# Two engines that read one PSUM buffer: both of ScalarE's copies ahead of VectorE's, small transfers spread over tiles, a mean computed later

## The chip, the cores and the metric

The kernel runs on one core of a Trainium2 chip. The metric is the device time of one execution, in microseconds (us). A core has the engines TensorE (PE, with PEld for its weight loads), VectorE (DVE), ScalarE (ACT), GpSimd (POOL) and SyncE (SP), which issues transfers. They run side by side, each in its own order, and wait for one another by semaphores.

## The reference

One layer of an encoder, on two sequences of 2048 tokens with 1024 features, with shared weights:

```
h = rms_norm(x, norm_w);  proj = h @ w_in
q_a, k_a, v_a, g_a, q_b, k_b, v_b, g_b = split(proj)     # 512 128 128 512 | 512 512 512 512
q_a, k_a = partial_rope(rms_norm(q_a)), partial_rope(rms_norm(k_a))
o_a = windowed_gqa_sink(q_a, k_a, v_a, sink_a) * silu(g_a)   # 8 q heads, 2 kv heads, +-128 tokens
q_b, k_b = rms_norm(q_b), rms_norm(k_b)
o_b = neighbourhood_attn(q_b, k_b, v_b, rpb_b) * silu(g_b)   # 8 heads, 64-wide grid, 8 x 16 window
x = x + concat(o_a, o_b) @ w_out
y = x + (p @ w_ple) * sigmoid(x @ w_ple_gate)
```

All of it is in fp32.

## The kernel before

Matmul operands are kept as two rounded parts: ScalarE writes the high part ("hi") of a value, VectorE the rest ("lo" = value − hi), and a product is three matmuls, hi·hi, hi·lo and lo·hi. So most results in PSUM are read by both engines: ScalarE copies or scales them into a high part, VectorE subtracts that high part from the same PSUM buffer.

The span has three stages. Stage A (0 to some 790 us) takes 32 tiles of 128 tokens, 16 of each sequence; `f` numbers them. For each tile `proj_a(f)` projects k and v (PSUM `pk`), q (`pq`) and the gate (`pg`), and two calls of `unit_a` (one for each kv head) do the windowed attention: scores `sc`, softmax (`mx`, `nm` and the exponentials L219 into `s`), transposes `pt` into PSUM and from there into `pr`, products `po`, and `fin`, which transposes the gate into `pgt`, adds the two halves of `po` into `ot` (L537 and L538) and multiplies (L539). Stage B (790 to some 1860 us) takes 64 tiles, `f` from 32 to 95: two halves of the heads, two sequences, 16 tiles each. `proj_b(f)` projects q and k together (`pqk`) and v and the gate together (`pvg`), `keys_b` transposes the keys into PSUM `pktb` and writes four blocks of `ks_b` from it, `prep_b` and `split_q` make `q1b` and `q`, and `unit_b` does the attention: `scb`, exponentials, `ptb` into `p_t`, products `pob`, and `fin` with `pgtb` and `o_tb` (added up on POOL at L694, multiplied on DVE at L697). Its products come in four blocks, `x` = 0 to 3. Behind stage B come the output projection and, in stage C, the gate's products, which the change does not touch.

TensorE's order is set by hand: `pinned` links every matmul and transpose to the one before, and `PLAN_A` and `PLAN_B` say at which share of the projection's work a step of the attention is put in. The order on the other engines is made by the scheduler from the program and its dependencies; SP's transfers and a few operations are kept in program order. Each engine then runs its list strictly in order, and an instruction that waits holds those behind it.

PSUM buffers come from pools by tag: three for the projections, three shared by `sc`, `scb`, `pt`, `ptb`, `pgt` and `pgtb`, and two shared by `pkt`, `pqt`, `po` and their counterparts of stage B. A new tile of a tag waits until the one that held its buffer has been read: the third `ptb` of a tile takes the buffer of `pgtb`, so it waits for `o_tb` L697.

`square(f, i)` squares one half of x for the row means: the load `stn<-x_n`, ScalarE's square in place (L292) and, behind the second half, VectorE's two small operations `ms` (L300) and `ee` (L302). `split(f, i)` makes the two parts of x itself (`xr` on ScalarE L278, then POOL L279). Both are called while TensorE is in an earlier tile's projection. `regroup(s)` runs after the last tile of a sequence in stage A: it writes the 2048 means to DRAM (L471) and reads them back in the order of stage B's tiles in 16 small transfers (L474); `stats_b(s)` turns them into scales. `raw` (L461) is a step of `combine`, which prepares sums of weights for stage C on POOL, one operation in some of stage B's tiles.

Of the kernel before, what the change touches and what calls it, by code (L numbers as in the profile page):

```python
# [11 lines left out]
F32 = mybir.dt.float32  # L12
# [7 lines left out]
DM = 1024  # L20
# [64 lines left out]
def emit(ctx, tc, io):  # L85
# [108 lines left out]
    def project(ps, xr, w, cost):  # L194

        for k in range(KT):
            for i, (a, b) in enumerate(((0, 0), (0, 1), (1, 0))):
                mm(ps, xr[:, a, k, :], w(k, b), k == 0 and i == 0, k == KT - 1 and i == 2)
                yield cost, k == KT - 1 and i == 2
# [32 lines left out]

    def split_q(pqt, q1, q2):

        for e in range(2):
            a, z = 64 * e, 64 - 64 * e
            nc.scalar.copy(q1[e][a:a + 64], pqt[a:a + 64])
            nc.vector.tensor_tensor(out=q2[e][a:a + 64], in0=pqt[a:a + 64], in1=q1[e][a:a + 64].bitcast(F32),
                                    op=ALU.subtract)
            nc.gpsimd.tensor_copy(q1[e][z:z + 64], q1[e][a:a + 64])  # L240
        return q1, q2


# [39 lines left out]
    def square(f, i):  # L283

        if f >= 2 * NT:
            return
        if i == 0:
            stats[f] = (ap.tile([128, 12], F32, tag="ssq", name="ssq", bufs=3),
                        ap.tile([128, 1], F32, tag="ee", name="ee", bufs=3))
        ssq, ee = stats[f]  # L290
        xn = staged.pop(("n", f, i))
        nc.scalar.activation(xn, xn, AF.Square, accum_out=ssq[:, 10 + i:11 + i])  # L292
        if f > 1:
            load_next()
        if i == 1:
            for dst, src in copies[:CP] if f >= 2 else ():
                tc.keep_in_program_order(nc.sync.dma_start(dst, src))
                copies.pop(0)
            ms = ms_a[:, f:f + 1]
            nc.vector.tensor_scalar(out=ms, in0=ssq[:, 10:11], scalar1=ssq[:, 11:12], scalar2=1.0 / DM,  # L300
                                    op0=ALU.add, op1=ALU.mult)
            nc.vector.tensor_scalar(out=ee, in0=ms, scalar1=EPS, scalar2=EPS * EPS, op0=ALU.mult, op1=ALU.add)  # L302

    def big(shape, dt, name):
        return ap.tile(shape, dt, tag="big", name=name, bufs=3)
# [60 lines left out]
    def keys_a(kt, t):  # L366
        pkt = ptile([128, 128], "ms", "pkt")
        tr(pkt, kt[:, 0:2, :].rearrange("p h d -> p (h d)"))
        c = slice(128 * t, 128 * t + 128)
        for e in range(2):  # L370
            a, z = 64 * e, 64 - 64 * e
            nc.scalar.activation(ks_a[a:a + 64, e, c], pkt[a:a + 64], AF.Copy, scale=wk[a:a + 64, 0:1])
            nc.vector.scalar_tensor_tensor(out=ks_a[z:z + 64, e, c], in0=pkt[a:a + 64], scalar=wk[a:a + 64, 0:1],
                                           in1=ks_a[a:a + 64, e, c].bitcast(F32), op0=ALU.mult, op1=ALU.subtract)

    def proj_a(f):
# [2 lines left out]
        ka = 22 if f in last else KA  # L379
        pk = ptile([128, 256], "pj", "pk")  # L380
        yield from project(pk, xr, lambda k, b: wx[:, k, b, :], 112)
        sq2 = ap.tile([128, 512], F32, tag="sq", name="sq2", bufs=2)
        nc.scalar.activation(sq2[:, :128], pk[:, 0:128], AF.Square)
        nc.vector.tensor_reduce(out=ssq[:, 8:10], in_=sq2[:, :128].rearrange("p (h d) -> p h d", d=HD),
# [56 lines left out]
        held[f] = q, gs, y  # L441
        if t == NT - 1:
            regroup(s)
        if f == NT + 4:
            stats_b(0)
        yield 0, False

# [21 lines left out]
    def regroup(s):  # L469
        c = slice(NT * s, NT * s + NT)  # L470
        nc.sync.dma_start(ms_d[s * SEQ:(s + 1) * SEQ].rearrange("(t p) -> p t", p=128), ms_a[:, c])  # L471
        rows = ms_d.rearrange("(r k c) -> r k c", k=4, c=16)
        for i in range(NT * s, NT * s + NT):
            nc.sync.dma_start(ms_b[:, i:i + 1], rows[8 * (i // 4):8 * (i // 4) + 8, i % 4, :].rearrange("r c -> c r"))  # L474

    def stats_b(s):
        c = slice(NT * s, NT * s + NT)
# [14 lines left out]
    def unit_a(f, kv):  # L492
        s, t = divmod(f, NT)
        _, gs, y = held[f]
        k0, k1 = max(0, t - 1), min(NT, t + 2)
        n = 128 * (k1 - k0)
        m0 = 128 * (k0 - t + 1)
        sm, prs, got = sm_tiles(), [], {}

        def sc(i):  # L500
            ps = ptile([128, 512], "sc", "sc")
            for j, q in enumerate(qs[f]):
                mm(ps[:, :n], q[kv][:, 128 * i:128 * i + 128], ks_a[:, kv, 128 * k0:128 * k1], j == 0, j == 1)
            softmax(i, ps, n, mask[:, m0:m0 + n], sm)
            if i == 3:
                got["g2"] = exps(sm, n, y[:, 11:12], gs[:, 256 * kv:256 * kv + 256],
                                 (snk[:, 0, 4 * kv:4 * kv + 4], snk[:, 1, 4 * kv:4 * kv + 4]))

        def pt(j):
            if j >= k1 - k0:  # L510
                return
            pt = ptile([128, 4, 128], "pt", "pt")
            for i in range(4):
                tr(pt[:, i, :], sm["s"][i][:, 128 * j:128 * j + 128])
            pr = main.tile([128, 2, 512], F32R, tag="p_t", name="pr", bufs=3)
            pf = pt.rearrange("p h q -> p (h q)")
            nc.scalar.copy(pr[:, 0], pf)
            nc.vector.tensor_tensor(out=pr[:, 1], in0=pf, in1=pr[:, 0].bitcast(F32), op=ALU.subtract)  # L518
            prs.append(pr)

        def po(j):
            if j == 0:
                got["po"] = ptile([128, 512], "ms", "po")
            if j < k1 - k0:
                v = vv[:, k0 + j, kv].rearrange("p a d -> p (a d)")
                for i in range(2):
                    mm(got["po"], v, prs[j][:, i], j == 0 and i == 0, k0 + j == k1 - 1 and i == 1)

        def fin(_):
            pgt = ptile([128, 2, 128], "sc", "pgt")  # L530
            for i in range(2):
                tr(pgt[:, i, :], got["g2"][:, 128 * i:128 * i + 128])
            ot = ap.tile([128, 2, 128], F32, tag="ot", name="ot", bufs=2)
            ph2 = got["po"].rearrange("p (i e q) -> p e i q", e=2, q=128)
            for e in range(2):
                a, z = 64 * e, 64 - 64 * e
                nc.scalar.copy(ot[a:a + 64], ph2[z:z + 64, e])  # L537
                nc.vector.tensor_tensor(out=ot[a:a + 64], in0=ph2[a:a + 64, e], in1=ot[a:a + 64], op=ALU.add)  # L538
            nc.vector.tensor_tensor(out=ot, in0=pgt, in1=ot, op=ALU.mult)  # L539
            nc.sync.dma_start(oa_d[s].rearrange("(i p) q -> p i q", p=128)[:, 2 * kv:2 * kv + 2, 128 * t:128 * t + 128],  # L540
                              ot)
        return {"sc": sc, "pt": pt, "po": po, "fin": fin, "prep": lambda _: nxt(f) if kv else None}
# [3 lines left out]
    def keys_b(kt, b, cb):  # L546
        pkt = ptile([128, 2, 16, 8], "ms", "pktb")
        for i in range(2):
            tr(pkt[:, i].rearrange("p c r -> p (c r)"), kt[:, 2 * i:2 * i + 2, :].rearrange("p h d -> p (h d)"))
        for i in range(2):  # L550
            for e in range(2):
                a, z = 64 * e, 64 - 64 * e
                hi, lo = (ks_b[i][p:p + 64, 8 * b:8 * b + 8, e, 16 * cb:16 * cb + 16].rearrange("p r c -> p c r")
                          for p in (a, z))
                nc.scalar.activation(hi, pkt[a:a + 64, i], AF.Copy, scale=wk[a:a + 64, 1:2])  # L555
                nc.vector.scalar_tensor_tensor(out=lo, in0=pkt[a:a + 64, i], scalar=wk[a:a + 64, 1:2],  # L556
                                               in1=hi.bitcast(F32), op0=ALU.mult, op1=ALU.subtract)

    def proj_b(f):
        half, st = divmod(f - 2 * NT, 2 * NT)  # L560
        s, j = divmod(st, NT)
        b, cb = divmod(j, 4)
        if f == 2 * NT + 4:
            stats_b(1)
        if not ks_b:
            ks_b.extend(big([128, 32, 2, 64], F32R, f"ks_b{i}") for i in range(2))
# [26 lines left out]
        for i, c in enumerate(project(pv, xr, lambda k, b: w_vg[k][:, b, :], 215)):  # L593
# [3 lines left out]
            if i == (KB if f not in last else 10):  # L597
                if f < 2 * NT + 2:
                    pending.append((kt, b, cb))
                else:  # L600
                    keys_b(kt, b, cb)
        v = ap.tile([128, 4, 2, HD], F32R, tag="sq", name="vb", bufs=2)
        vp = pv[:, 0:256].rearrange("p (h d) -> p h d", d=HD)
        nc.scalar.activation(v[:, :, 0, :], vp, AF.Copy, scale=rs_b[:, st:st + 1])
        nc.vector.scalar_tensor_tensor(out=v[:, :, 1, :], in0=vp, scalar=rs_b[:, st:st + 1],
                                       in1=v[:, :, 0, :].bitcast(F32), op0=ALU.mult, op1=ALU.subtract)
        for w, (c0, ncol) in COL_WIN.items():
            lo, hi = max(c0, 16 * cb), min(c0 + ncol, 16 * cb + 16)
            if lo < hi:
                nc.sync.dma_start(v_d[half, s, w][8 * b:8 * b + 8, lo - c0:hi - c0].rearrange("r c h a d -> c r (h a d)"),  # L610
                                  v[8 * (lo - 16 * cb):8 * (hi - 16 * cb)].bitcast(F32).rearrange("p h a d -> p (h a d)"))
        gs = qg[:, 1].rearrange("p h d -> p (h d)")
        nc.scalar.activation(gs, pv[:, 256:512], AF.Tanh, scale=hr_b[:, st:st + 1])
        nc.vector.scalar_tensor_tensor(out=gs, in0=gs, scalar=1.0, in1=pv[:, 256:512], op0=ALU.add, op1=ALU.mult)
        held[f] = qg[:, 0], gs
        next(combining, None)
# [526 lines left out]
```

## Time and profile before

| | |
|---|---|
| median of three runs | 2642.3 us (2638.67, 2642.3, 2643.25) |
| profiled execution | 2645.63 us |
| its span | 2643.9 us |
| granted clock of TensorE in it | 0.988 of full speed |

The span is what the profiler saw from the first to the last instruction; the profiled execution's own time is 1.7 us above it. "Busy" is the time in which an engine executes; waits are put down to what released them. A row of the timeline has the start in us from the beginning of the span, the duration, the engine, the line, the operation, output and inputs, and in brackets the idle time ahead of it. The lines are quoted in the prediction.

### The profile page before, as it was taken

The numbers are of one execution on the slowest core, as the hardware profiler recorded it, in microseconds if no ns is written. First come the engines' busy times: TensorE is split into PE (matmuls) and PEld (weight loads), VectorE is DVE, ScalarE is ACT, GpSimd is POOL, SyncE is SP. The second block draws the span as 40 slices with busy tenths as digits, with TensorE's granted clock in tenths as the row PEclk, the third lists the DMA queues.
The fourth block names the chain that finished last, engine by engine and source line by source line (L and its number), as shares of the span: only waits on it lengthen the run. The fifth ranks groups of instructions, "written<-read, shape, count | busy, mean of one in ns | idle before, by whom it ended". The sixth has DMA issues, their size and how long they took to land.

```text
span 2643.9 us, 46984 instructions
## 1 busy us (share of the span) xinstructions
PE 2559.5 (97%) x16080; PEld 2274.8 (86%) x16080; DVE 1927.4 (73%) x5702; ACT 1419.9 (54%) x3327; POOL 794.5 (30%) x996
## 2 busy tenths in 40 slices
PE   7999989999999999999899999999979998999999
PEld 5888878888877888888788888888979998999999
DVE  5887778878797788888888888888675548555554
ACT  5666656666665566666666666666431124222322
POOL 3332323333232333333333332221132323223321
PEclk9999999999999999999999999999989999999999
DMA  6323322111133455555755554457575455233221
GB/s 203 106 94 108 106 75 77 61 59 49 53 101 117 157 174 170 180 177 158 235 164 168 188 175 145 152 156 220 172 244 176 151 172 179 76 104 101 81 78 48
DMA packets 230974, 357.50 MB, mean 135 GB/s; under 512 B 38320, under 2 KB 115760, under 8 KB 225584
## 3 DMA queue, kind: packets, MB, share of 16 engines
q1 hardware_dynamic: 230736, 354.51, 42.7%
q8 instruction: 128, 2.10, 0.3%
q14 instruction: 110, 0.90, 0.1%
HBM read 266.33 MB, written 105.92 MB: 141 GB/s over the span
## 4 chain that ended last, share of the span: by engine, by line
PE 67%; DVE 13%; ACT 9%; DMA 5%; issue 3%; POOL 2%; SPq 1%; DVEq 0%; POOLq 0%; ACTq 0%
PE pqk L189 12%; PE pvg L189 12%; PE acca L973 11%; PE accc L973 8%; ACT s L219 4%; PE pob L189 4%; PE pple L189 3%; PE scb L189 3%; PE ptb L192 3%; DMA stn<-x_n 3%; PE pout L189 3%; DVE s L204 2%; DVE pr L518 2%; PE pq L189 2%; PE pg L189 1%
## 5 line engine op out<-in xcount | busy, mean ns | idle before, releaser
L189 PE MATMUL pvg<-wb,xr 128*128 128x512 f32 x1536 | 457.8, 405 | 0.0
L189 PE MATMUL pqk<-wa,xr 128*128 128x512 f32 x1536 | 436.8, 407 | 0.0
L219 ACT ACTIVATE s<-s,nm 128x384 f32<-128x384 f32 (+4 forms) x512 | 306.3, 600 | 242.0 <-DVE nm L215 183.1
L189 PEld LDWEIGHTS pqk<-wa,xr 128*128 128x128 f32 x1536 | 266.8, 189 | 37.2
L189 PEld LDWEIGHTS pvg<-wb,xr 128*128 128x128 f32 x1536 | 269.1, 190 | 31.6
L279 POOL TENSOR_TENSOR xr<-stx,xr 128x512 fp32r<-128x512 f32 x192 | 248.1, 1300 | 143.1 <-ACT xr L278 125.5
L189 PE MATMUL pg<-wb,xr 128*128 128x512 f32 x768 | 232.4, 409 | 1.5 <-ACT wb L142 0.9
L189 PE MATMUL pq<-wa,xr 128*128 128x512 f32 x768 | 224.3, 406 | 5.4 <-DVE wa L143 2.8
L229 POOL TENSOR_TENSOR g<-qg,rd 128x256 f32<-128x256 f32 x64 | 39.2, 613 | 492.8 <-DVE rd L227 478.9
L973 PE MATMUL acca<-opd,s 128*128 128x256 f32 x1344 | 171.1, 290 | 16.6 <-DVE r L992 13.1
L973 PEld LDWEIGHTS acca<-opd,s 128*128 128x128 f32 x1344 | 169.2, 199 | 17.1 <-DVE r L992 10.1
L189 PEld LDWEIGHTS pq<-wa,xr 128*128 128x128 f32 x768 | 142.1, 192 | 30.3 <-DVE wa L143 3.8
L204 DVE CUSTOM_DVE_ANT_0 s<-scb,bias 128x288 f32<-128x288 f32 (+3 forms) x256 | 141.9, 555 | 30.0 <-PE scb L189 25.2
L667 ACT CAST p_t<-ptb 96x384 fp32r<-96x384 f32 (+3 forms) x256 | 129.8, 508 | 51.4 <-PE ptb L192 49.7
L189 PEld LDWEIGHTS pg<-wb,xr 128*128 128x128 f32 x768 | 137.1, 189 | 23.0 <-DVE wb L143 1.8
L668 DVE TENSOR_TENSOR p_t<-ptb,p_t 96x384 fp32r<-96x384 f32 (+3 forms) x256 | 149.0, 584 | 9.1 <-ACT p_t L667 6.2
L555 ACT ACTIVATE ks_b<-pktb,wk 64x128 fp32r<-64x128 f32 x256 | 124.9, 489 | 47.9 <-DVE ks_b L556 41.6
L189 PEld LDWEIGHTS pob<-p_t,vw 128*128 128x128 f32 (+2 forms) x832 | 132.8, 189 | 18.9 <-ACT wa L142 0.5
L556 DVE SCALAR_TENSOR_TENSOR ks_b<-pktb,wk,ks_b 64x128 fp32r<-64x128 f32 x256 | 115.0, 449 | 39.7 <-ACT ks_b L555 33.1
L939 POOL TENSOR_TENSOR opd<-sum,opd 128x1024 fp32r<-128x1024 f32 x28 | 70.2, 2508 | 235.9 <-ACT opd L925 235.9
L189 PE MATMUL pob<-p_t,vw 128*128 128x256 f32 (+2 forms) x832 | 140.4, 282 | 0.1
L204 DVE CUSTOM_DVE_ANT_0 s<-sc,mask 128x384 f32<-128x384 f32 (+1 forms) x256 | 136.2, 534 | 0.2
(197 smaller groups left out, 5878.6 us busy)
## 6 DMA issues: line engine op xcount, KB each, us to landing
stx<-x_b SPq DMA_DIRECT2D x128, 256.0 KB
vw<-v_d SPq DMA_DIRECT2D x112, 256.0 KB
stx<-x_a SPq DMA_DIRECT2D x64, 256.0 KB
stn<-x_n SPq DMA_DIRECT2D x64, 256.0 KB
v_d<-vb SPq DMA_DIRECT2D x64, 256.0 KB
x1r<-x_d SPq DMA_DIRECT2D x16, 1024.0 KB
y_t<-r SPq DMA_DIRECT2D x64, 256.0 KB
v_d<-vb SPq DMA_DIRECT2D x96, 128.0 KB
```

Source lines behind the costliest of these rows:

```text
L189: pinned(nc.tensor.matmul(out, lhsT, rhs, start=start, stop=stop))
L192: pinned(nc.tensor.transpose(out, in_, ident))
L204: nc.vector.tensor_tensor_reduce(out=s[:, :n], in0=ps[:, :n], in1=bias, scale=1.0, scalar=-3.0e38, op0=ALU.add, op1=ALU.max, accum_out=sm[ ...
L219: nc.scalar.activation(ss[i][:, :n], ss[i][:, :n], AF.Exp, bias=nm[:, i:i + 1], accum_out=den[:, i:i + 1])
L279: nc.gpsimd.tensor_tensor(out=lo, in0=raw, in1=hi.bitcast(F32), op=ALU.subtract)
L518: nc.vector.tensor_tensor(out=pr[:, 1], in0=pf, in1=pr[:, 0].bitcast(F32), op=ALU.subtract)
L555: nc.scalar.activation(hi, pkt[a:a + 64, i], AF.Copy, scale=wk[a:a + 64, 1:2])
L556: nc.vector.scalar_tensor_tensor(out=lo, in0=pkt[a:a + 64, i], scalar=wk[a:a + 64, 1:2], in1=hi.bitcast(F32), op0=ALU.mult, op1=ALU.subtract)
L667: nc.scalar.copy(p_t[:kc, :nch, 0], pf)
L668: nc.vector.tensor_tensor(out=p_t[:kc, :nch, 1], in0=pf, in1=p_t[:kc, :nch, 0].bitcast(F32), op=ALU.subtract)
L939: each(lambda x, y, z: eng.tensor_tensor(out=x, in0=y, in1=z, op=ALU.subtract), out, a, b)
L973: pinned(nc.tensor.matmul(ps[:, kk], w[k][:, a, c:c + 128], o[:, b, k], start=i in (0, 1, 4) and kk == 0 and k == 0 and j == 0, stop=k == ...
```

## The change

Four parts. (1) Where ScalarE and VectorE read one PSUM buffer in halves or quarters, ScalarE now makes all of its copies first and VectorE its subtractions or additions behind them: `split_q`, `keys_a`, `fin` of `unit_a`, `keys_b`; in `proj_b` the Tanh of the gate follows ScalarE's `vb`. (2) The 16 reads of `regroup` are put in a list and two of them are issued in each of the next eight tiles; `stats_b` moves five tiles back. (3) `ms` and `ee` move from `square` to `proj_a`, behind the projection `pk`. (4) Nothing else: the instructions are the same in kind and number, and the order on TensorE is the same.

```diff
     def split_q(pqt, q1, q2):
-        for e in range(2):
-            a, z = 64 * e, 64 - 64 * e
-            nc.scalar.copy(q1[e][a:a + 64], pqt[a:a + 64])
-            nc.vector.tensor_tensor(out=q2[e][a:a + 64], in0=pqt[a:a + 64], in1=q1[e][a:a + 64].bitcast(F32),
-                                    op=ALU.subtract)
-            nc.gpsimd.tensor_copy(q1[e][z:z + 64], q1[e][a:a + 64])
+        ends = [(e, slice(64 * e, 64 * e + 64), slice(64 - 64 * e, 128 - 64 * e)) for e in range(2)]
+        for e, a, _ in ends:
+            nc.scalar.copy(q1[e][a], pqt[a])
+        for e, a, z in ends:
+            nc.vector.tensor_tensor(out=q2[e][a], in0=pqt[a], in1=q1[e][a].bitcast(F32), op=ALU.subtract)
+            nc.gpsimd.tensor_copy(q1[e][z], q1[e][a])
...
     def square(f, i):
-            ms = ms_a[:, f:f + 1]
-            nc.vector.tensor_scalar(out=ms, in0=ssq[:, 10:11], scalar1=ssq[:, 11:12], scalar2=1.0 / DM,
-                                    op0=ALU.add, op1=ALU.mult)
-            nc.vector.tensor_scalar(out=ee, in0=ms, scalar1=EPS, scalar2=EPS * EPS, op0=ALU.mult, op1=ALU.add)
...
     def proj_a(f):
         yield from project(pk, xr, lambda k, b: wx[:, k, b, :], 112)
+        nc.vector.tensor_scalar(out=ms, ...)      # the two operations of square
+        nc.vector.tensor_scalar(out=ee, ...)
...
         if t == NT - 1:
             regroup(s)
-        if f == NT + 4:
+        else:
+            regroup_next()
+        if f == NT + 9:
             stats_b(0)
...
     def regroup(s):
-        for i in range(NT * s, NT * s + NT):
-            nc.sync.dma_start(ms_b[:, i:i + 1], rows[8 * (i // 4):8 * (i // 4) + 8, i % 4, :].rearrange("r c -> c r"))
+        regroups.extend((ms_b[:, i:i + 1], rows[8 * (i // 4):8 * (i // 4) + 8, i % 4, :].rearrange("r c -> c r"))
+                        for i in range(NT * s, NT * s + NT))
+    def regroup_next():
+        for dst, src in regroups[:2]:
+            tc.keep_in_program_order(nc.sync.dma_start(dst, src))
+        del regroups[:2]
...
         def fin(_):                                   # of unit_a
             for e in range(2):
                 a, z = 64 * e, 64 - 64 * e
                 nc.scalar.copy(ot[a:a + 64], ph2[z:z + 64, e])
+            for e in range(2):
+                a = 64 * e
                 nc.vector.tensor_tensor(out=ot[a:a + 64], in0=ph2[a:a + 64, e], in1=ot[a:a + 64], op=ALU.add)
...
     def keys_b(kt, b, cb):                            # keys_a alike, with two copies
-        for i in range(2):
-            for e in range(2):
-                ...
-                nc.scalar.activation(hi, pkt[a:a + 64, i], AF.Copy, scale=wk[a:a + 64, 1:2])
-                nc.vector.scalar_tensor_tensor(out=lo, in0=pkt[a:a + 64, i], scalar=wk[a:a + 64, 1:2],
-                                               in1=hi.bitcast(F32), op0=ALU.mult, op1=ALU.subtract)
+        for i, a, hi, _ in parts:
+            nc.scalar.activation(hi, pkt[a:a + 64, i], AF.Copy, scale=wk[a:a + 64, 1:2])
+        for i, a, hi, lo in parts:
+            nc.vector.scalar_tensor_tensor(out=lo, in0=pkt[a:a + 64, i], scalar=wk[a:a + 64, 1:2],
+                                           in1=hi.bitcast(F32), op0=ALU.mult, op1=ALU.subtract)
...
     def proj_b(f):
-        if f == 2 * NT + 4:
+        if f < 2 * NT + 8:
+            regroup_next()
+        if f == 2 * NT + 9:
             stats_b(1)
...
+        gs = qg[:, 1].rearrange("p h d -> p (h d)")
         nc.scalar.activation(v[:, :, 0, :], vp, AF.Copy, scale=rs_b[:, st:st + 1])
+        nc.scalar.activation(gs, pv[:, 256:512], AF.Tanh, scale=hr_b[:, st:st + 1])
         nc.vector.scalar_tensor_tensor(out=v[:, :, 1, :], in0=vp, scalar=rs_b[:, st:st + 1], ...)
...
-        gs = qg[:, 1].rearrange("p h d -> p (h d)")
-        nc.scalar.activation(gs, pv[:, 256:512], AF.Tanh, scale=hr_b[:, st:st + 1])
         nc.vector.scalar_tensor_tensor(out=gs, in0=gs, scalar=1.0, in1=pv[:, 256:512], op0=ALU.add, op1=ALU.mult)
```

What the scheduler makes of it, at three places. First VectorE in a tile of stage B, from the addition of the previous tile's heads (`otb`) to the third `p_t`; `ks_b` are the four low parts of the keys, `qg` the normalised q (from `pqk`) or the gate (from `pvg`), `q_212` the low part of q. Before:

```order
L687 TENSOR_TENSOR otb<-pob,otb 64x512
L588 TENSOR_TENSOR qg<-pqk,yb 128x256
L238 TENSOR_TENSOR q_212<-pqtb,q1b 64x256
L697 TENSOR_TENSOR o_tb<-pgtb,o_tb 128x256
L668 TENSOR_TENSOR p_t<-ptb,p_t 128x3x128
L238 TENSOR_TENSOR q_212<-pqtb,q1b 64x256
L556 SCALAR_TENSOR_TENSOR ks_b_10370<-pktb,wk,ks_b_10370 64x16x8
L605 SCALAR_TENSOR_TENSOR vb<-pvg,rs_b,vb 128x4x64
L668 TENSOR_TENSOR p_t<-ptb,p_t 128x3x128
L556 SCALAR_TENSOR_TENSOR ks_b_10370<-pktb,wk,ks_b_10370 64x16x8
L614 SCALAR_TENSOR_TENSOR qg<-qg,pvg 128x256
L668 TENSOR_TENSOR p_t<-ptb,p_t 128x3x128
```

After:

```order
L701 TENSOR_TENSOR otb<-pob,otb 64x512
L602 TENSOR_TENSOR qg<-pqk,yb 128x256
L239 TENSOR_TENSOR q_208<-pqtb,q1b 64x256 x2
L711 TENSOR_TENSOR o_tb<-pgtb,o_tb 128x256
L682 TENSOR_TENSOR p_t<-ptb,p_t 128x3x128
L568 SCALAR_TENSOR_TENSOR ks_b_10356<-pktb,wk,ks_b_10356 64x16x8 x2
L568 SCALAR_TENSOR_TENSOR ks_b_10357<-pktb,wk,ks_b_10357 64x16x8 x2
L621 SCALAR_TENSOR_TENSOR vb<-pvg,rs_b,vb 128x4x64
L628 SCALAR_TENSOR_TENSOR qg<-qg,pvg 128x256
L682 TENSOR_TENSOR p_t<-ptb,p_t 128x3x128 x3
```

All four `ks_b`, `vb` and the gate now stand ahead of the second `p_t`; before, one `ks_b` and `vb` did. ScalarE's list in the same tile has the same shape: both `q1b`, the first `p_t`, `vb`, four `ks_b`, the Tanh, then the second `p_t`. VectorE's first `ks_b` waits for the last of ScalarE's four.

POOL in such a tile; `g` scales the gate, `xr` is the low part of x. Before:

```order
L229 TENSOR_TENSOR g_15456<-qg,rd 128x256
L240 COPY q1b<-q1b 64x256
L694 TENSOR_TENSOR o_tb<-otb 128x2x16x8
L240 COPY q1b<-q1b 64x256
L461 TENSOR_TENSOR raw<-raw 128x512
L279 TENSOR_TENSOR xr<-stx,xr 128x512 x2
```

After, the same tile:

```order
L229 TENSOR_TENSOR g_15456<-qg,rd 128x256
L240 COPY q1b<-q1b 64x256 x2
L464 TENSOR_TENSOR raw<-raw 128x512
L708 TENSOR_TENSOR o_tb<-otb 128x2x16x8
L279 TENSOR_TENSOR xr<-stx,xr 128x512 x2
```

`o_tb` now stands behind the second copy and, in 22 of the 64 tiles, behind `raw` as well.

ScalarE in stage A, from the exponentials of one unit to the next transposes' copies; `q_5113` and `q_5114` are the high parts of q, `gs` is the Tanh of the gate. Before:

```order
L219 ACTIVATE s,den<-s,nm 128x384 x4
L224 ACTIVATE es<-es 128x4
L537 COPY ot<-po 64x256
L237 CAST q_5113<-pqt 64x512
L439 ACTIVATE gs<-pg,y 128x512
L537 COPY ot<-po 64x256
L278 CAST xr<-stx 128x512
L237 CAST q_5114<-pqt 64x512
L517 CAST pr<-pt 128x512
```

After:

```order
L219 ACTIVATE s,den<-s,nm 128x384 x4
L224 ACTIVATE es<-es 128x4
L548 COPY ot<-po 64x256 x2
L237 CAST q_7042<-pqt 64x512
L237 CAST q_7043<-pqt 64x512
L440 ACTIVATE gs<-pg,y 128x512
L278 CAST xr<-stx 128x512
L528 CAST pr<-pt 128x512
```

The second copy of `ot` no longer stands behind the copy of q and the Tanh.

More of the change, by code (lines that the diff above doesn't have):

```diff
@@ L370, in keys_a @@
         for e in range(2):
+            a = 64 * e
+            nc.scalar.activation(ks_a[a:a + 64, e, c], pkt[a:a + 64], AF.Copy, scale=wk[a:a + 64, 0:1])
+        for e in range(2):
             a, z = 64 * e, 64 - 64 * e
-            nc.scalar.activation(ks_a[a:a + 64, e, c], pkt[a:a + 64], AF.Copy, scale=wk[a:a + 64, 0:1])
             nc.vector.scalar_tensor_tensor(out=ks_a[z:z + 64, e, c], in0=pkt[a:a + 64], scalar=wk[a:a + 64, 0:1],
@@ L381, in proj_a @@
         yield from project(pk, xr, lambda k, b: wx[:, k, b, :], 112)
+        nc.vector.tensor_scalar(out=ms, in0=ssq[:, 10:11], scalar1=ssq[:, 11:12], scalar2=1.0 / DM,
+                                op0=ALU.add, op1=ALU.mult)
+        nc.vector.tensor_scalar(out=ee, in0=ms, scalar1=EPS, scalar2=EPS * EPS, op0=ALU.mult, op1=ALU.add)
         sq2 = ap.tile([128, 512], F32, tag="sq", name="sq2", bufs=2)
@@ L472, in regroup @@
         rows = ms_d.rearrange("(r k c) -> r k c", k=4, c=16)
-        for i in range(NT * s, NT * s + NT):
-            nc.sync.dma_start(ms_b[:, i:i + 1], rows[8 * (i // 4):8 * (i // 4) + 8, i % 4, :].rearrange("r c -> c r"))
+        regroups.extend((ms_b[:, i:i + 1], rows[8 * (i // 4):8 * (i // 4) + 8, i % 4, :].rearrange("r c -> c r"))
+                        for i in range(NT * s, NT * s + NT))
+    regroups = []
+    def regroup_next():
+        for dst, src in regroups[:2]:
+            tc.keep_in_program_order(nc.sync.dma_start(dst, src))
+        del regroups[:2]
     def stats_b(s):
@@ L537, in fin @@
                 nc.scalar.copy(ot[a:a + 64], ph2[z:z + 64, e])
+            for e in range(2):
+                a = 64 * e
                 nc.vector.tensor_tensor(out=ot[a:a + 64], in0=ph2[a:a + 64, e], in1=ot[a:a + 64], op=ALU.add)
@@ L549, in keys_b @@
             tr(pkt[:, i].rearrange("p c r -> p (c r)"), kt[:, 2 * i:2 * i + 2, :].rearrange("p h d -> p (h d)"))
-        for i in range(2):
-            for e in range(2):
[L552 to L556, printed above, removed]
-                                               in1=hi.bitcast(F32), op0=ALU.mult, op1=ALU.subtract)
+        parts = [(i, 64 * e, *(ks_b[i][p:p + 64, 8 * b:8 * b + 8, e, 16 * cb:16 * cb + 16].rearrange("p r c -> p c r")
+                               for p in (64 * e, 64 - 64 * e))) for i in range(2) for e in range(2)]
+        for i, a, hi, _ in parts:
[3 more added lines that the diff above has]
+                                           in1=hi.bitcast(F32), op0=ALU.mult, op1=ALU.subtract)
     def proj_b(f):
```

## The prediction

> **What bounds the kernel now.** I read the page first, then the waits of TensorE stage by stage, then single tiles in the timeline.
>
> ```profile
> span 2643.9 us, 46984 instructions
> PE 2559.5 (97%) x16080; PEld 2274.8 (86%) x16080; DVE 1927.4 (73%) x5702; ACT 1419.9 (54%) x3327; POOL 794.5 (30%) x996
> PE 67%; DVE 13%; ACT 9%; DMA 5%; issue 3%; POOL 2%; SPq 1%; DVEq 0%; POOLq 0%; ACTq 0%
> ```
>
> TensorE works for 97% of the span, and its own order is written out by hand, so it is the wall; the other engines matter only where one of its instructions stands and waits. Those waits follow for stage A (0 to 790 us; engine, line, released by: total, times, longest), and behind the dots for stage B (790 to 1860 us) with two waits between ScalarE and VectorE.
>
> ```profile
> PE pt L192 <- DVE ot L539: 12.8, 21, 2.0
> PE pt L192 <- ACT s L219: 6.8, 3, 6.0
> PEld pt L192 <- DVE ot L539: 19.2, 24, 2.1
> ...
> PE scb L189 <- DVE mx L204: 4.9, 2, 3.6
> ACT ks_b L555 <- DVE ks_b L556: 41.6, 71, 2.6
> DVE ks_b L556 <- ACT ks_b L555: 33.1, 68, 0.7
> ```
>
> In stage A the `pt` transposes wait for the end of the gated head output `ot` again and again; the `PEld` row is the same wait seen from the weight loads (24 times, 0.8 us each). In stage B TensorE waits for almost nothing: its largest wait is 4.9 us in 1070 us. The last two rows are what the change is aimed at: for `ks_b` ScalarE stands 41.6 us for VectorE and VectorE 33.1 us for ScalarE, in turns. But neither row is a wait of TensorE.
>
> **The change, part by part.** No instruction is added or removed; TensorE's order is the same. What counts is when DVE, ACT and POOL reach the instruction that a TensorE instruction waits for.
>
> *The copies of `ot` in stage A.* The end of one unit's `fin`:
>
> ```profile
> 498.17 0.37 ACT L537 COPY ot<-po 64x256 f32<-64x256 f32 x1
> 499.02 0.36 ACT L537 COPY ot<-po 64x256 f32<-64x256 f32 x1 [0.48 <-DVE ot L538]
> 499.42 0.43 DVE L538 TENSOR_TENSOR ot<-po,ot 64x256 f32<-64x256 f32 x1 [0.29 <-ACT ot L537]
> 499.95 0.42 DVE L539 TENSOR_TENSOR ot<-pgt,ot 128x256 f32<-128x256 f32 x1
> 500.43 0.66 PE L192 MATMUL pt<-ident,s 128*128 128x128 f32 x4 [0.34 <-DVE ot L539]
> ```
>
> The second copy is held 0.48 us by the first addition though it reads the other half of the partitions. Copied one behind the other, the second addition waits only for the first one; L539 comes about 0.43 us earlier, and the 0.34 us stall is covered. In the other unit of a tile the order on ACT has the copy of q and the Tanh between the two `ot` copies before, and not after, so more than 0.43 us goes there. Lower bound: 21 waits at no more than 0.43 us, 9 us; upper bound: all 19.2 of the PEld row. I take 16, nearer the upper end, since half of the units lose the two instructions in between as well. What is late next: the exponentials L219, which wait for x's second read (below). `split_q` and `keys_a` are regrouped in the same way; no TensorE wait on them is among those of stage A, so they give and cost nothing there: the rest of a projection runs between their transposes and their use.
>
> *The regrouped means, and the mean made where it is used.*
>
> ```profile
> 339.23 0.59 SPq L474 DMA_DIRECT2D ms_b<-ms_d  x1
> 341.01 10.26 SPq L474 DMA_DIRECT2D ms_b<-ms_d  x15
> 351.36 0.53 SPq L261 DMA_DIRECT2D stn<-x_n  x1
> ...
> ACT stn L292 <- DMA stn<-x_n: 87.1, 56, 10.6
> DVE ms_a L300 <- ACT stn L292: 37.7, 28, 9.3
> ...
> 357.83 1.67 PE L192 MATMUL pt<-ident,s 128*128 128x128 f32 x3 [6.05 <-ACT s L219]
> ```
>
> SP issues the 16 small reads without a break (10.26 us for 15, 0.68 each); the load `stn` stands behind them, ScalarE waits 10.6 us for it with the exponentials queued behind the square, and TensorE stands 6.05 us. Two reads per tile are 1.4 us of a tile of over 20 us, and go ahead of the loads without holding one long. SP's issue time is the same in total. Gain: 6 us, bounds 0 (the stall moves to another load) and 6.8 us (the whole wait on `s`). In stage B two reads on SP in each of eight tiles stand ahead of loads with no TensorE wait. A second burst stands at the end of the other sequence's tiles; of the 6.8 us of waits on `s`, 6.0 are one wait, so that one gives nothing. Moving L300/L302 behind the `pk` projection takes a wait of 37.7 us off VectorE; the exponentials' `nm` comes ahead of it, but the square that this wait was for still runs ahead of the exponentials on ScalarE. I put it at 0 (bounds −3 to +3, some 0.1 us in each of 32 tiles).
>
> Stage A together: −22 us (bounds −9 and −26).
>
> *Keys and queries in stage B.* This is where a price appears. One tile of before; x0 = 1412.31, the first copy of `q1b`:
>
> ```profile
> 1412.31 0.37 ACT L237 CAST q1b<-pqtb 64x256 fp32r<-64x256 f32 x1
> 1412.91 0.39 POOL L240 CAST q1b<-q1b 64x256 fp32r<-64x256 f32 x1
> 1413.38 0.74 POOL L694 TENSOR_TENSOR o_tb<-otb 128x256 f32<-128x256 f32 x1
> 1413.68 0.47 ACT L667 CAST p_t<-ptb 96x384 fp32r<-96x384 f32 x1 [1.00 <-PE ptb L192]
> 1414.16 0.42 DVE L697 TENSOR_TENSOR o_tb<-pgtb,o_tb 128x256 f32<-128x256 f32 x1 [0.37 <-POOL o_tb L694]
> 1414.50 0.54 DVE L668 TENSOR_TENSOR p_t<-ptb,p_t 96x384 fp32r<-96x384 f32 x1
> 1414.57 0.47 ACT L604 ACTIVATE vb<-pvg,rs_b 128x256 fp32r<-128x256 f32 x1
> 1414.94 0.48 ACT L555 ACTIVATE ks_b<-pktb,wk 64x128 fp32r<-64x128 f32 x1
> 1415.15 1.29 POOL L461 TENSOR_TENSOR raw<-raw 128x512 f32<-128x512 f32 x1
> 1415.21 0.65 ACT L278 CAST xr<-stx 128x512 fp32r<-128x512 f32 x1
> 1415.54 0.44 DVE L556 SCALAR_TENSOR_TENSOR ks_b<-pktb,wk,ks_b 64x128 fp32r<-64x128 f32 x1
> 1415.59 0.49 PE L192 MATMUL ptb<-ident,s 128*96 128x128 f32 x3
> 1416.01 0.48 DVE L605 SCALAR_TENSOR_TENSOR vb<-pvg,rs_b,vb 128x256 fp32r<-128x256 f32 x1
> 1416.41 0.54 DVE L668 TENSOR_TENSOR p_t<-ptb,p_t 96x384 fp32r<-96x384 f32 x1
> 1417.47 0.42 DVE L614 SCALAR_TENSOR_TENSOR qg<-qg,pvg 128x256 f32<-128x256 f32 x1
> 1417.81 0.55 DVE L668 TENSOR_TENSOR p_t<-ptb,p_t 96x384 fp32r<-96x384 f32 x1
> 1418.92 0.52 PE L189 MATMUL pob<-p_t,vw 96*128 96x256 f32 x3
> ...
> 1428.65 0.37 ACT L237 CAST q1b<-pqtb 64x256 fp32r<-64x256 f32 x1
> 1431.52 0.49 PE L192 MATMUL ptb<-ident,s 128*128 128x128 f32 x3
> 1434.85 0.51 PE L189 MATMUL pob<-p_t,vw 128*128 128x256 f32 x3
> ```
>
> In this tile TensorE asks for two things: the third `ptb` at 1415.59 (x0 + 3.28) takes the buffer of `pgtb`, which DVE's `o_tb` must have read (it had at 1414.58), and the second `pob` of the head pair at 1418.92 (x0 + 6.61) reads the second `p_t`, whose DVE half was ready at 1416.95, 2 us early. The last three rows show a tile where the two stand at x0 + 2.87 and x0 + 6.20. After the change both come later.
>
> POOL makes both `q1b` copies (12.91, and 0.47 behind it 13.38) ahead of `o_tb`, which then starts at 13.85 and ends at 14.60; DVE's `o_tb` ends at 15.06. That alone is hidden. But in 22 of the 64 tiles the order puts `raw`, 1.29 us, ahead of `o_tb` too: it starts at 15.10 (raw to the next `xr` takes 1.25), and DVE's `o_tb` ends at 16.30, x0 + 4.05 with a hand-over of 0.06 (as from 500.37 to 500.43 above). The third `ptb` waits 0.77 us here and 1.18 us in the other tile.
>
> The second `p_t` is issued behind all four `ks_b`, `vb` and `qg`. ScalarE: first `p_t` 13.68, `vb` 14.05, first `ks_b` 0.37 on at 14.42, the next three 0.27 apart (14.94 to the `xr` at 15.21 shows that step), the last ends at 15.71. VectorE's first `ks_b` waits for that last one (this is a new wait: it did wait for the first), so it starts at 15.77. The four go 0.47 apart (15.54 to 16.01), `vb` at 17.65, `qg` 0.40 later, `p_t` 0.34 behind that (17.47 to 17.81), at 18.39, and 0.54 long: ready at 18.99 with the hand-over, x0 + 6.68, against 6.61 and 6.20. Stall 0.07 to 0.48, mean 0.28, in each of the 42 tiles without `raw`: 11.8 us. In the 22 others VectorE's first `p_t` starts behind `o_tb`, at 16.22, `ks_b` 0.57 later (its 0.54 and the 0.03 by which 0.47 exceeds 0.44), and the second `p_t` is ready at x0 + 7.70; the `pob`, moved by the first stall to x0 + 7.38, waits 0.32 more: 1.09 and 1.50, mean 1.3, together 28.6. Sum for stage B: +40 us.
>
> Bounds: if VectorE's `ks_b` went as close as 0.36 us apart (its `qg` to `p_t`, 0.34, is the nearest row), the 0.28 and 0.32 vanish and 22 × 0.98 = 22 us is left. If ScalarE's four copies went a whole duration apart (0.48 for 0.27), the last ends 0.6 us later, which the tiles with `raw` hide and the others pay: 42 × 0.88 + 28.6 = 66 us. I take 40, since both steps it rests on are seen in the tile itself.
>
> One rule of the Trainium skill bears on this. By "VectorE: DVE Perf Modes", section "Two Vector instructions with no wait between them", a Vector instruction whose input or output starts in another group of 32 partitions than that of the one before is held until every earlier one has finished. The four `ks_b` change halves from one to the next, so by it they would not overlap and go a duration apart; the trace agrees as far as it goes, 0.47 us from `ks_b` to `vb` at a duration of 0.44. By the rule stage B costs the 40 us, and if it did not hold here, the 22.
>
> The Tanh moved ahead frees the `pvg` buffer earlier, and the freed waits between ACT and DVE (41.6 and 33.1 us) shorten their queues; TensorE waits for neither now, so both count 0.
>
> **The sum.** 2645.6 us (the profiled execution: span 2643.9 and 1.7 around it) − 22 + 40 = 2663.6. That execution lies 3.3 us above the median of the three runs, 2642.3, so against the median: 2660 us, +0.7%.
>
> **The rivals.**
>
> *Stage B hides it; only the gain of stage A is left (faster).* It decides at the second `p_t`: were it ready before x0 + 6.2, and `o_tb` before x0 + 2.87, nothing in B would wait. For it: the 74.7 us of turn-taking between ACT and DVE go, and 2 us were in hand. Against it: the order itself, four `ks_b`, `vb` and `qg` (2.6 us) ahead of `p_t`, and `raw` ahead of `o_tb`. It gives 2642.3 − 22 = 2620. With B at its lower bound, 22, it would not yet be faster.
>
> *The two cancel.* B at 22 and A at −22: 2642. A gain near −26 with the 22, or 40 with a larger saving than I can see, stays within 5.3 us.
>
> *The gain in A does not come.* The exponentials wait for the square, which waits for `stn`; these waits are 87.1 us in 56 places, 1.6 each, and an `ot` that is 0.43 us earlier uncovers them. Against it: the `pt` waits name `ot`, with `s` only once at length. Gain 9, cost 40: 2673.
>
> *The change does not do what it says.* The two means stay nearly in their place (behind `nm` in the order, not behind the projection), which alters neither sum.
>
> **How the numbers follow.** Forecast (B costs 30 to 66, A gives 15 or more): 0.50. A gives less than that, B costs: 0.13; both are slower. Cancelled: 0.15. B hidden: 0.22. Changes under 0.2% (5.3 us) can't be told from none for this kernel. So slower 0.63, same 0.15, faster 0.22. The range: from 2638 (A −26, B +22) down to 2632, to take in part of the hidden case, up to 2682 (A −22, B +62); the forecast's own is 2646 (A −26, B +30) to 2693 (A −15, B +66), whose far corner needs both bounds at once.
>
> **What the profile afterwards would show.** `pt <- ot` down from 12.8 us to under 5, and no 6 us wait on `s` near 358: right for A. New waits of TensorE in stage B, on DVE `o_tb` (about 1 us in some 22 tiles) and on DVE `p_t` (0.1 to 0.5 in most): right for B. A tile with `raw` should be 1.1 to 1.5 us longer from `q1b` to `q1b`. If `pob` waits for nothing, the `ks_b` went faster than 0.47 each; if the third `ptb` doesn't, POOL did `raw` elsewhere. If stage A keeps its waits under another name, the third rival holds. The prediction is wrong if stage B ends less than 20 us later relative to its start.

## The result, and the profile after

The changed kernel took 2687.27 us (median; 2683.67 to 2689.2) against 2640.49 us beside it: ratio 1.0172, interval 1.0159 to 1.0184, so 1.7% or some 46 us slower. The direction was forecast, and the two places in stage B where TensorE stands; the size was not: 2660 with a range to 2682.

The page of the changed kernel, as it was shown of the one before:

```profile
span 2687.4 us, 46925 instructions
PE 2574.7 (96%) x16080; PEld 2263.5 (84%) x16080; DVE 1922.6 (72%) x5702; ACT 1419.4 (53%) x3327; POOL 792.1 (29%) x996
PE 58%; DVE 20%; ACT 8%; DMA 6%; issue 5%; POOL 3%; SPq 0%; DVEq 0%; POOLq 0%; ACTq 0%
```

DVE and ACT are busy for about as long as before (1927.4 and 1419.9 us): the work itself costs no more. But the chain that ended last now runs through DVE for 20% of the span, 13% before. TensorE's waits in stage A, and behind the dots in stage B:

```profile
PE pt L192 <- DVE ot L552: 6.7, 8, 3.0
PE sc L189 <- DVE pr L529: 6.2, 24, 1.6
...
PE ptb L192 <- DVE o_tb L711: 21.3, 22, 1.3
PE pob L189 <- DVE p_t L682: 18.7, 34, 1.2
```

In stage A `pt` on `ot` is down from 21 waits and 12.8 us to 8 waits and 6.7 us (the forecast had under 5), and the 6 us wait on `s` is gone, as forecast; new are 24 waits of `sc` on `pr`. In stage B, which had no wait of note, stand the two that were forecast.

A wait view leaves out what a wait costs around it, so the kernels are compared below by the start of the same TensorE instruction in each trace (their order is the same): the difference to before at the first `pvg` of stage B (786.5 us before) is the yield of stage A, and how it changes up to the 63rd `pvg` tile (1801.8 us before) is the price of stage B. A minus sign means earlier than before. The first three columns are us, each from one profiled execution; the last is from the times of all runs.

| kernel (the experiments below) | at the start of B | at tile 63 | stage B alone | ratio of times, interval |
|---|---|---|---|---|
| changed kernel | −16.4 | +43.9 | +60.3 | 1.0172 (1.0159–1.0184) |
| keys_turns | −14.7 | +18.5 | +33.2 | 1.0061 (1.0048–1.0073) |
| split_turns | −20.8 | +46.3 | +67.1 | 1.0162 (1.0148–1.0176) |
| both_turns | −20.6 | −18.8 | +1.8 | 0.9919 (0.9906–0.9933) |
| keys_halves | −13.0 | +29.6 | +42.6 | 1.0103 (1.0089–1.0117) |
| split_turns_halves | −19.7 | +8.8 | +28.5 | 1.0022 (1.0012–1.0032) |
| raw_narrow | −17.7 | −3.4 | +14.3 | 0.9985 (0.9976–0.9994) |
| only_regroup | −2.6 | −0.7 | +1.9 | 0.9974 (0.9963–0.9984) |
| only_ot | −14.2 | −12.2 | +2.0 | 0.9940 (0.9926–0.9954) |
| only_ms | +2.1 | +1.0 | −1.1 | 0.9997 (0.9988–1.0006) |
| ot_and_regroup | −20.7 | −21.0 | −0.3 | 0.9902 (0.9888–0.9915) |

Against −22 and +40 of the forecast, the changed kernel has −16.4 and +60.3. A tile of stage B without `raw`, x0 = 1641.27:

```profile
1641.27 0.76 ACT L237 CAST q1b<-pqtb 64x256 fp32r<-64x256 f32 x2
1642.63 0.47 ACT L681 CAST p_t<-ptb 96x384 fp32r<-96x384 f32 x1 [0.60 <-PE ptb L192]
1643.04 0.47 ACT L619 ACTIVATE vb<-pvg,rs_b 128x256 fp32r<-128x256 f32 x1
1643.41 1.97 ACT L566 ACTIVATE ks_b<-pktb,wk 64x128 fp32r<-64x128 f32 x4
...
1645.42 1.84 DVE L568 SCALAR_TENSOR_TENSOR ks_b<-pktb,wk,ks_b 64x128 fp32r<-64x128 f32 x4 [0.37 <-ACT ks_b L566]
1648.02 1.48 DVE L682 TENSOR_TENSOR p_t<-ptb,p_t 96x384 fp32r<-96x384 f32 x3
...
1648.62 0.62 PE L189 MATMUL pob<-p_t,vw 96*128 96x256 f32 x3 [0.57 <-DVE p_t L682]
```

Up to `vb` and the first `ks_b` (x0 + 2.14; the forecast had 2.11) ScalarE is where it was expected. Then its four `ks_b` take 1.97 us, not 1.29. They go 0.49 apart, a whole duration, where 0.27 was taken; the last ends at x0 + 4.11 instead of 3.40, VectorE stands 0.37 us for it, and `pob` starts at x0 + 7.35, where the forecast had 6.68.

### The profile page after: what moved, and what is told of

It reads as the page before. It is cut to its first block, busy times and chain, and to the rows that moved or that the text cites. A ratio compares the mean times of both kernels' runs of the same rounds, so it can differ in the third digit from the quotient of the medians.

```text
span 2687.4 us, 46925 instructions
## 1 busy us (share of the span) xinstructions
PE 2574.7 (96%) x16080; PEld 2263.5 (84%) x16080; DVE 1922.6 (72%) x5702; ACT 1419.4 (53%) x3327; POOL 792.1 (29%) x996
## 4 chain that ended last, share of the span: by engine, by line
PE 58%; DVE 20%; ACT 8%; DMA 6%; issue 5%; POOL 3%; SPq 0%; DVEq 0%; POOLq 0%; ACTq 0%
PE acca L987 11%; PE accc L987 8%; PE pvg L189 8%; PE pqk L189 6%; PE pq L189 4%; ACT s L219 4%; PE pple L189 3%; DVE ks_b L568 3%; PE scb L189 3%; PE pob L189 3%; PE pg L189 3%; DVE s L204 2%; PE pout L189 2%; PE sc L189 2%; PE po L189 2%
## 5 line engine op out<-in xcount | busy, mean ns | idle before, releaser
L189 PEld LDWEIGHTS pob<-p_t,vw 128*128 128x128 f32 (+2 forms) x832 | 127.1, 189 | 59.2 <-DVE p_t L682 46.9
L189 PE MATMUL pob<-p_t,vw 128*128 128x256 f32 (+2 forms) x832 | 146.3, 289 | 19.8 <-DVE p_t L682 18.7
L192 PE MATMUL ptb<-ident,s 128*128 128x128 f32 (+2 forms) x832 | 133.8, 274 | 23.0 <-DVE o_tb L711 22.2
L192 PEld LDWEIGHTS ptb<-ident,s 128*128 128x128 f32 (+2 forms) x832 | 100.6, 136 | 60.3 <-issue 36.3
L682 DVE TENSOR_TENSOR p_t<-ptb,p_t 96x384 fp32r<-96x384 f32 (+3 forms) x256 | 139.9, 582 | 6.3 <-ACT p_t L681 4.9
```

Of the source, the lines that this page charges most:

```text
L189: pinned(nc.tensor.matmul(out, lhsT, rhs, start=start, stop=stop))
L192: pinned(nc.tensor.transpose(out, in_, ident))
L682: nc.vector.tensor_tensor(out=p_t[:kc, :nch, 1], in0=pf, in1=p_t[:kc, :nch, 0].bitcast(F32), op=ALU.subtract)
```

## The experiments

Unless another kernel is named, an edit is to the changed kernel. The waits called "start to start" here and in the expectations are TensorE's start of an instruction less that of the one before it and less what the pair takes without a wait; they include the weight load, and so are larger than the wait view's.

**Keys in turns again.**

```diff
-        for i, a, hi, _ in parts:
-            nc.scalar.activation(hi, ...)
-        for i, a, hi, lo in parts:
-            nc.vector.scalar_tensor_tensor(out=lo, ...)
+        for i in range(2):
+            for e in range(2):
+                ...
+                nc.scalar.activation(hi, ...)
+                nc.vector.scalar_tensor_tensor(out=lo, ...)
```

> The changed kernel with keys_b alone written in turns again (ScalarE, VectorE, ScalarE, VectorE). Theory: the second p_t is then no longer behind four ks_b, so TensorE's waits of pob on p_t (28.7 us in the changed kernel, counted start to start) vanish and those of ptb on o_tb (25 us, 22 tiles with raw ahead of o_tb) stay: 2687 - 29 = 2658 us. Rival, the second p_t is late because of the copies of q and raw ahead of it, not because of ks_b: the pob waits stay and the time is within 5 us of 2687.

```profile
PE ptb L192 <- DVE o_tb L712: 23.0, 23, 1.4
PE scb L189 <- DVE mx L204: 4.6, 3, 2.7
```

2661.65 us, as the theory had it. These are the two largest waits of stage B: `pob` on `p_t` is out of the list, `ptb` on `o_tb` is untouched. So the second `p_t` is late because of the grouped keys: with the queries still grouped and the keys not, `pob` no longer waits for it.

**The queries in turns again.**

```diff
-        for e, a, _ in ends:
-            nc.scalar.copy(q1[e][a], pqt[a])
-        for e, a, z in ends:
-            nc.vector.tensor_tensor(...); nc.gpsimd.tensor_copy(...)
+        for e in range(2):
+            nc.scalar.copy(...); nc.vector.tensor_tensor(...); nc.gpsimd.tensor_copy(...)
```

> The changed kernel with split_q alone written in turns again; o_tb then stands ahead of raw on GpSimd. Theory: the waits of ptb on o_tb (25 us, 22 tiles) vanish, but in those tiles the second p_t is then as late as in the others, 0.88 us instead of 0.45 behind ks_b: net 22 x 0.6 = 13 us less, 2674 us, with the waits of pob on p_t up from 28.7 to some 45 us. Rival, the two waits are independent: all 25 us come back, 2662 us.

A miss of both: 2688.08 us, no gain at all. The waits on `o_tb` did vanish, but those on `p_t` rose to 53.6 us by the wait view, 62.8 start to start:

```profile
PE pob L189 <- DVE p_t L682: 53.6, 55, 1.6
...
1429.43 0.37 ACT L237 CAST q1b<-pqtb 64x256 fp32r<-64x256 f32 x1
1430.81 0.48 ACT L681 CAST p_t<-ptb 96x384 fp32r<-96x384 f32 x1 [1.01 <-PE ptb L192]
1431.31 0.37 ACT L237 CAST q1b<-pqtb 64x256 fp32r<-64x256 f32 x1
1432.08 1.96 ACT L566 ACTIVATE ks_b<-pktb,wk 64x128 fp32r<-64x128 f32 x4
1434.07 1.84 DVE L568 SCALAR_TENSOR_TENSOR ks_b<-pktb,wk,ks_b 64x128 fp32r<-64x128 f32 x4 [1.44 <-ACT ks_b L566]
1437.28 0.62 PE L189 MATMUL pob<-p_t,vw 96*128 96x256 f32 x3 [1.06 <-DVE p_t L682]
```

The second `q1b` copy goes back between the first `p_t` and `vb`, ahead of the keys, so ScalarE's group ends at x0 + 4.61 (x0 = 1429.43), 0.50 later than in the tile above, and `pob` starts at x0 + 7.85, also 0.50 later. VectorE waits 1.44 us for the fourth copy: the wait that the grouping added is what ends last here. The two grouped parts hide part of each other's price, which is why undoing the keys alone took off 29 us and undoing the queries alone next to nothing.

**Both in turns again**, with both edits above.

> The changed kernel with split_q and keys_b in turns again; the regrouped fin of unit_a, keys_a, the spread transfers and the moved mean stay. Theory: stage B is as before but for the transition into it, and only the gain of stage A is left, 16.4 us at the first projection of stage B: 2640 - 16 = 2624 us, 2629 if the 5 us that the changed kernel loses in the first four tiles of stage B stay. Rival, stage B also loses by the spread transfers or by the moved Tanh: 2640 or more.

2622.9 us, ratio 0.9919. Stage B alone costs 1.8 us, so neither the spread transfers nor the Tanh costs anything to speak of there. Grouping keys and queries is the loss; the rest of the change gains 0.8%. It also showed a price that was not forecast: stage A yields 20.8 us in split_turns and 16.4 in the changed kernel, 20.6 here and 14.7 in keys_turns, and each pair differs in the grouped queries alone. The 24 waits of `sc` on `pr` look like the reason and are not. Stage A of split_turns:

```profile
PE sc L189 <- POOL xr L279: 6.3, 24, 0.4
...
PE pt L192 <- DVE ot L552: 3.4, 7, 1.6
```

With the queries in turns `sc` waits as often and as long (6.3 us, 6.2 in the changed kernel), only for `xr`. Even in only_ot below, where the queries are as before, the `sc` behind the projection of q take 6.9 us more start to start: these waits come with the earlier `ot`. What the grouped queries take back is at `pt`, which waits 6.7 us for `ot` in the changed kernel and 3.4 in split_turns; start to start, the `pt` that follow the gate's projection take 5.9 us more there than in split_turns. Why `ot` comes later with grouped queries was not traced.

**The keys by halves.** The blocks of both engines in the order lower, lower, upper, upper half of the partitions instead of lower, upper, lower, upper.

```diff
-        ... for i in range(2) for e in range(2)]
+        ... for e in range(2) for i in range(2)]
```

> The changed kernel with the four blocks of ks_b in another order: the two that read partitions 0 to 63 first, then the two that read 64 to 127, so that neighbours share their half except once; nothing else is changed. Theory: on ScalarE as on VectorE an instruction that starts on another half of the partitions than the one before it doesn't overlap it (0.49 us from ks_b to ks_b in the changed kernel, against 0.27 from ks_b to xr where the half is the same). Then the four copies take 1.5 us instead of 1.95, VectorE's four 1.65 instead of 1.85, and the stall of pob on p_t falls by some 0.6 us in 42 tiles and 0.2 in 22: 2687 - 28 = 2659 us. Rival, a copy of 64 partitions takes 0.49 us wherever it starts: no change, 2687 us.

```profile
PE ptb L192 <- DVE o_tb L711: 21.4, 23, 1.3
PE pob L189 <- DVE p_t L682: 6.3, 19, 0.4
...
1600.20 1.48 ACT L566 ACTIVATE ks_b<-pktb,wk 64x128 fp32r<-64x128 f32 x4
1602.51 1.64 DVE L568 SCALAR_TENSOR_TENSOR ks_b<-pktb,wk,ks_b 64x128 fp32r<-64x128 f32 x4
```

The groups shrank to what the theory gave (1.5 and 1.65), 1.48 and 1.64 us. Start to start, the medians over 62 tiles are 0.27, 0.47 and 0.29 us on ScalarE (0.49, 0.50 and 0.49 in the changed kernel) and 0.36, 0.45 and 0.36 on VectorE (0.46, 0.47 and 0.46). The short steps are those at which the half stays, and the rival falls. The time fell by less than the 28 us expected: 0.7% by the ratios, 18 us. The likely reason is that VectorE waited only 0.37 us for ScalarE in the changed kernel, not the 0.49 that ScalarE saved.

**The same where VectorE waits longer**: the order of halves, with the queries in turns, to test that reason.

> The kernel of split_turns (split_q in turns, keys_b grouped) with the blocks of ks_b in the order of keys_halves: both of the lower half of the partitions, then both of the upper. In split_turns VectorE's first ks_b starts at the end of ScalarE's fourth (1.44 us of idle ahead of it), so both shorter groups count in full, 0.49 us on ScalarE and 0.21 on VectorE, in all 55 tiles in which pob waits for p_t. Theory: 62.8 - 55 x 0.70 = 24 us of those waits are left, 2688 - 38 = 2650 us. Rival, the gain of keys_halves, 15 us, is all that the order of the halves can give, wherever VectorE waits: 2673 us.

```profile
PE pob L189 <- DVE p_t L682: 18.2, 47, 1.1
```

2650.27 us, where 2650 was expected; start to start 26 us of waits are left of 62.8. Where ScalarE's group is what ends last, its shortening counts in full.

**The GpSimd operation ahead of `o_tb`**, an edit to the kernel of keys_turns. It leaves out most of the sums of weights that stage C needs, so only its time is of use:

```diff
-                    tc.keep_in_program_order(nc.gpsimd.tensor_tensor(out=out, in0=a, in1=b, op=op))
+                    tc.keep_in_program_order(nc.gpsimd.tensor_tensor(out=out[:, :64], in0=a[:, :64], in1=b[:, :64], op=op))
```

> The kernel of keys_turns (the changed kernel with keys_b in turns), with the raw operations on GpSimd cut to 64 of their 512 columns; the order of all engines stays. This leaves out most of the sums of weights for stage C. Theory: raw, 1.28 us ahead of o_tb in 22 tiles, is what the third ptb waits for; at some 0.35 us o_tb comes 0.95 us earlier and the waits of ptb on o_tb fall from 26.8 us to under 3 us: 2662 - 24 = 2638 us, 0.997 of before. Rival, the two copies of q1b ahead of o_tb are enough to make it late: the waits stay above 15 us.

```profile
PE ptb L192 <- DVE o_tb L712: 1.9, 6, 0.5
```

2639.88 us, with 23.0 us of waits down to 1.9. So it is `raw` that makes `o_tb` late, and the two copies of `q1b` ahead of it are hidden by themselves. A loss of 14 us from the start of stage B to tile 63 stays. Start to start, 6.5 us of it are at the third `ptb`, nearly all in tiles with a `raw`, which still takes 0.32 us ahead of `o_tb`; the rest is in small steps and was not traced.

**One part alone, added to the kernel before**: the spread transfers, the two copies of `ot`, and the moved mean, each as in the change's diff.

> The kernel before with the spread transfers alone (two reads per tile, stats_b five tiles later). Theory: the stall of TensorE near 358 us goes, 8 to 9 us by the milestones of the changed kernel, nothing else moves: 2645 - 8 = 2637 us, 0.997 of before. Rival, the stall moves to a later load: 2645 us.

> The kernel before with the two copies of ot one behind the other in fin of unit_a, and nothing else. Theory: the rest of the gain of stage A is from here, 20.6 us in both_turns less the 9 of the transfers: 2645 - 11 = 2634 us, 0.996 of before, and the waits of pt on ot fall from 12.8 us to some 4. Rival, the gain needs the moved mean as well: the waits of pt on ot stay above 8 us and the time within 5 us of before.

> The kernel before with the two small operations of the mean moved behind the projection pk, and nothing else. Theory: TensorE waits for neither, so the time is that of before within 2 us, 2645 us. Rival, VectorE's 37.7 us of waits for the square held the exponentials: 5 to 10 us less.

TensorE's wait on `ot` in stage A with the transfers alone (on `s` 0.3 us are left of 6.8), then two of its waits in only_ot, then VectorE's wait with only the mean moved:

```profile
PE pt L192 <- DVE ot L549: 16.6, 28, 2.6
...
PE pt L192 <- ACT s L219: 5.3, 3, 4.8
PE pt L192 <- DVE ot L541: 3.8, 5, 2.0
...
DVE ms_a L378 <- ACT stn L292: 38.3, 29, 7.3
```

The transfers: 2638.81 us, 0.9974, as expected. In the profile 8 us are gained around 360 us, and the waits on `ot` grow from 12.8 to 16.6 us behind it, so part is given back there. (The profiled execution, 2643.21 us, was one of the slowest of the nine, so the table's row shows less than the ratio.) The copies of `ot`: 2628.85 us, 0.9940, 16 us where 11 were expected, and 3.8 us of waits left of 12.8; 14.2 us of it stand at the start of stage B. The mean: 2644.76 us against 2644.8 before, nothing; VectorE waits for the square as long as before (38.3 us, 37.7 before), at the operation's new place.

**The two parts that gain, and nothing else.**

> The kernel before with the two copies of ot one behind the other and the spread transfers, and nothing else: the two parts that gained by themselves (only_ot 0.994, only_regroup 0.9974). Theory: their gains add up, 16 and 7 us: 2645 - 23 = 2622 us, 0.9914 of before, as both_turns (0.9919), which has the moved mean and the regrouped keys_a besides. Rival, both take the same waits: 0.994.

```profile
span 2615.9 us, 46992 instructions
```

2618.43 us, ratio 0.9902: 1% faster than before and 2.7% faster than the changed kernel (0.9902 / 1.0172). The gains add up, within the intervals.

## Why the prediction was right or wrong

*Right: where it is lost.* The second `p_t` behind the grouped keys and `o_tb` behind `raw` are the two large losses; keys_turns, both_turns and raw_narrow show each by taking its cause away. In a tile with `raw` of the changed kernel, x0 = 1431.98:

```profile
1433.51 1.28 POOL L464 TENSOR_TENSOR raw<-raw 128x512 f32<-128x512 f32 x1
1434.75 0.75 POOL L708 TENSOR_TENSOR o_tb<-otb 128x256 f32<-128x256 f32 x1
1435.53 0.42 DVE L711 TENSOR_TENSOR o_tb<-pgtb,o_tb 128x256 f32<-128x256 f32 x1 [1.63 <-POOL o_tb L708]
1436.10 0.50 PE L192 MATMUL ptb<-ident,s 128*96 128x128 f32 x3 [0.67 <-DVE o_tb L711]
1439.66 0.62 PE L189 MATMUL pob<-p_t,vw 96*128 96x256 f32 x3
```

The third `ptb` stands at x0 + 4.12 and `pob` at x0 + 7.68; the forecast had 4.05 and 7.70. The tiles with `raw` ahead were priced right, since `o_tb` ends last there.

*Wrong: "the next three 0.27 apart (14.94 to the `xr` at 15.21 shows that step)".* This is the step that failed. The row is that of a `ks_b` copy of the lower half followed by an instruction that starts at the same partition. Between two `ks_b` copies the half changes, and two rows of the trace of before have that case:

```profile
1416.24 0.49 ACT L555 ACTIVATE ks_b<-pktb,wk 64x128 fp32r<-64x128 f32 x1
1416.76 0.47 ACT L613 ACTIVATE qg<-pvg,hr_b 128x256 f32<-128x256 f32 x1
```

Here the copy is one of the upper half, and `qg` starts 0.52 us behind it. With 0.49 for 0.27 the tiles without `raw` pay 0.88 us each instead of 0.28, and stage B comes to the prediction's upper bound, 42 × 0.88 + 28.6 = 66 us, against the 60.3 measured. Tile by tile, from one `pvg` to the next, the 31 tiles in which no `raw` runs take 0.87 us more than before (median), the 31 others, most of which have it ahead of `o_tb`, 1.37; the forecast had 0.28 and 1.3: the working held, its input did not. The rule of the Trainium skill that was weighed ("VectorE: DVE Perf Modes", section "Two Vector instructions with no wait between them") held on VectorE, 0.46 us with a change of half and 0.36 without; it was not asked of ScalarE, where the same happened.

*Wrong in size: −22 us for stage A.* The two terms were not far off: ot_and_regroup has 20.7 us at the start of B for the forecast 16 + 6. (The 26 us of its ratio hold 6.6 more that come behind tile 63; no term of the forecast is about them, and their cause was not traced.) The step that was wrong is that `split_q` and `keys_a` "give and cost nothing there": the grouped `split_q` takes 4 to 7 us back in stage A (4.4, 5.9 and 6.7 by the three pairs of kernels that differ in it alone), at the `pt` that wait for `ot`; `keys_a` was not undone by itself.

*Right at nothing:* the moved mean, and the Tanh and the freed turn-taking in stage B: of the 74.7 us of waits between ScalarE and VectorE for `ks_b`, 19.3 are left in the changed kernel and 68.4 in both_turns, and it is both_turns whose stage B is within 1.8 us of before's. TensorE waited for none of them.

*The rivals.* "Stage B hides it" and "the two cancel" fell by the 60 us of stage B, against nothing and 22; "the gain in A does not come" fell, since 16.4 us came where it had 9, though the earlier `ot` did uncover other waits, those of `sc`. That the means stay nearly in place altered nothing, as the prediction said. The sum of stages A and B is +44 at tile 63, close to the ratio's 46.

## What to carry to other kernels

Grouping one engine's work ahead of another's takes away waits between the two, but puts the whole group ahead of whatever else stands in their queues; before doing so, look for what the bounding engine takes from those queues next and how early it is ready (here 2 us for `p_t` and 1 us for `o_tb`). When a step's price is taken from the distance of two instructions, take a pair with the same partitions as in the new order. Parts of one change can hide each other's price, so undo them one by one and also together: here the parts left over made the kernel 1% faster.

## What the runs showed of the hardware

On ScalarE, consecutive 64-partition copies of 128 columns from PSUM start 0.27 to 0.29 us apart when they read the same half of the partitions, and 0.47 to 0.50 us, their whole duration, when the half changes (medians over 62 tiles of keys_halves and of the changed kernel). VectorE's counterparts do the same: 0.36 and 0.45 to 0.47 us. Only the order of the four blocks differs between the two kernels.
